# Shorter GpSimd pieces in the setup of an mLSTM and attention trunk, and a scale-and-shift bound behind the attention's last low part

## The chip, the cores and the metric

The kernel runs on one core of one Trainium2 chip. The metric is the device time of one execution in microseconds (us); a version's time is the median over several runs.

## The reference

Two layers over a residual stream x of 1024 tokens by 1024 features, float32. Layer A is an mLSTM block, layer B attends over one shared set of keys and values.

```python
def mlstm_layer(x, w_in, conv_w, conv_b, wq, wk, wv, w_if, b_if, gn_g, skip, w_out):
    xm, z, o_pre = jnp.split(x @ w_in, 3, axis=-1)           # 3 x 2048 columns
    xc = jax.nn.silu(causal_dwconv(xm, conv_w, conv_b))
    q, k, v = headwise(xc, wq), headwise(xc, wk), headwise(xm, wv)   # 4 x 4 blocks
    gates = jnp.concatenate([q, k, v], axis=-1) @ w_if + b_if
    ...                                                       # chunkwise mLSTM, 4 heads of 512
    y = (h.astype(x.dtype) + skip * xc) * jax.nn.silu(z)
    return y @ w_out

def dilated_attention_layer(x, w_in, w_out, kv_blocks, slopes):
    ...          # 3 groups (windows 128, 512, 2048; dilations 1, 4, 16), 8 heads of 128, ALiBi
    o = jnp.sum(wts[..., None] * jnp.stack(outs), axis=0)     # groups merged by their softmax sums
    y = o.astype(x.dtype) * jax.nn.silu(z)
    return y @ w_out

# reference(): after each layer
x = layer_norm(ALPHA * x + y, ln_g[layer], ln_b[layer])
# after layer A the stream is projected once to K and V for all groups
```

## The kernel before

**Products.** Every large product is done in three passes: an operand is split into a high part (ScalarE casts it, line 93) and a low part (VectorE subtracts the high part, line 94), and TensorE multiplies high by high, high by low and low by high (lines 98, 99, 100). The projections use a Strassen-like scheme (`strassen_steps`, `strassen_wide`): a weight matrix comes in four quarters, VectorE forms sums of them (lines 246, 250, 263, 264, 314), each sum or quarter is split and multiplied, and VectorE joins the results (lines 227, 233, 318). One 128-row product of such a scheme is 12 matmuls of 128x512.

**Order.** The program is traced once, top to bottom. A scheduler then sets the order of every engine's queue: at each moment of its own estimated timeline it takes, of the instructions of an engine that are ready, the one traced first. Work that is traced later but ready sooner slips ahead. The engines work off their queues strictly in that order, so an instruction that waits holds up all that stand behind it. `tc.issue_after(ins)` takes this freedom away: what is traced in its block on the engine of `ins` is queued behind `ins`. All DMAs are issued by SyncE (SP).

**Memory.** On-chip memory is cut by hand into 53 slots of 4 KB per partition (`self.slot(i)`). A new tile in a slot has to wait for the last reader or writer of the old one, DMAs included.

**The setup's tables.** In layer A, `setup()` runs beside the first projections. GpSimd builds there the block-diagonal matrices for v (`spread`, line 424, with 7, 7 and 2 columns of 128) and, three times, the product of a head-wise weight with the gate weights (`through`: line 431 multiplies, lines 432 and 433 add). The three times share one slot, 51, so the third load (`in_wifr`) waits until the second is done. ScalarE then copies the third result, eight columns at a time, into 16 tables (`A.copy` at line 461), which the first `values` matmuls of layer A (line 608) read. `setup_scores()`, some 300 us later, calls `through` once and `spread` twice with 8 columns, for the matrix that takes the place of q and k in layer A.

**The stored rows.** Layer A ends with a LayerNorm without its gain and shift; the eight row blocks of 128 tokens are kept in DRAM as layer B's residual, and need gain and shift (`scale_row`, lines 950 and 951, two VectorE instructions of 128x1024). Blocks 0 to 3 are treated in layer A. Blocks 4 to 7 are treated in layer B by `residual(tb)`: load into slot 52 (line 1098), scale, shift, store (line 1100). Gain and shift (`gain0`) lie in slots 50 and 51.

**Layer B's loop.** For each half of the heads (quad), each group g and each head h of the half: `queries_keys` (a Strassen scheme for q and k), `scores`, `attend`, in that order; `values(g, quad)` makes a group's values first, and `gates(1)` stands ahead of the third group's. `residual(4 + h)` is called for h = 0 to 3 at the end of each head of the second group (g = 1):

```python
qk = queries_keys(h, g, weigh_late)
p = scores(h, g, qk, stats[h])
...
kept[h] = attend(h, g, p, head_values(g, v, h % 4, h == 4))
if (quad, g) == (0, 1):
    residual(4 + h)
```

In this group `attend` transposes the softmax weights for four residues r (line 1286), splits each result straight from its bank (a low part of 128x256 on VectorE, line 94) and multiplies them with v (lines 98 to 100, and line 1309 for a part that isn't split). `self.last_split` is the low part that was traced last, so at the call it is that of r = 3 of this head. The group also keeps q and k whole for a part of the scores, in the same slot 52 (`whole`, written at line 1213, read at line 1261). After the fourth head, `values(2, 0)` loads eight blocks of value weights (line 1163), the first two into slots 50 and 51, the third into slot 52.

Of the kernel before, what the change touches and what calls it, by code (L numbers as in the profile page):

```python
# [14 lines left out]
ALU = mybir.AluOpType  # L15
# [3 lines left out]
P = 128  # L19
# [4 lines left out]
NC_A = INNER // P  # L24
# [37 lines left out]
class Kernel:  # L62
# [358 lines left out]

    def spread(self, dst, src, n):

        self.nc.gpsimd.tensor_tensor(dst.rearrange("p c (n j) -> p c n j", j=4),
                                     src.unsqueeze(2).to_broadcast([P, n, 32, 4]),
                                     self.mask.unsqueeze(1).unsqueeze(3).to_broadcast([P, n, 32, 4]), op=ALU.mult)

    def through(self, dst, w, rep, m):

        G = self.nc.gpsimd  # L430
        G.tensor_tensor(rep, rep, w.unsqueeze(3).to_broadcast([P, NC_A, 4, m]), op=ALU.mult)
        G.tensor_tensor(rep[:, :, 0:2], rep[:, :, 0:2], rep[:, :, 2:4], op=ALU.add)
        G.tensor_tensor(dst, rep[:, :, 0], rep[:, :, 1], op=ALU.add)

    def setup(self):
# [649 lines left out]
    def layer_b(self):  # L1085
        nc, tc, a, cp = self.nc, self.tc, self.a, self.cp
        V, A, G, T = nc.vector, nc.scalar, nc.gpsimd, nc.tensor
# [7 lines left out]
        def residual(tb):  # L1095

            r = self.slot(52)
            nc.sync.dma_start(r, self.dram["x1", tb])
            self.scale_row(r, *gain0)
            nc.sync.dma_start(self.dram["x1", tb], r)  # L1100

        jt = self.const("jt", [P, 384], tag="k1")
# [362 lines left out]
        gain0 = []  # L1465
# [45 lines left out]
        for quad in range(2):  # L1511
# [3 lines left out]
            for g in range(3):  # L1515
                if (quad, g) in gate_at:
                    self.w_raw = raw2
                    for n, _ in enumerate(gates(gate_at[quad, g], qk_slots[1::2])):
                        if n == 3:
                            weigh_late(h + 1)  # L1520
                v = values(g, quad)
                for h in heads:
                    qk = queries_keys(h, g, weigh_late)
                    p = scores(h, g, qk, stats[h])
                    if h == 7 and g == 2:
                        y6 = weigh_late(8)
                    if (quad, g) == (1, 0) and h < 7:
                        with self.tc.issue_after(self.last_split.ins):
                            fourth(h - 4)
                    if g == 2:  # L1530
                        if h == 7:
                            works = 44
                        fac = factors(h, stats[h])
# [3 lines that stand above are left out]
                    if g == 2:  # L1537
                        merge(h, *fac)
                        if late:
                            merged = h  # L1540
                        elif h < 7:
                            late = fetch_late(h)
# [8 lines left out]
        r = lambda i: self.slot(i, dtype=F32R)  # L1551
# [3 lines left out]
        for c in range(HB):  # L1555
# [12 lines left out]
            if c >= 6:  # L1568
                for i in range(2):
                    cs = slice(512 * i, 512 * i + 512)  # L1570
# [138 lines left out]
```

## Time and profile before

| | |
|---|---|
| median of 3 runs | 2009.45 us (2007.83 to 2010.1) |
| the profiled execution | 2008.7 us; its span, first to last instruction, 2006.9 us |
| mean granted TensorE clock | 0.994 |
| busy share | TensorE 98%, VectorE 72%, ScalarE 50%, GpSimd 8% |
| `spread` in `setup()`, from 90.31 us | 2 x 128x896 and 1 x 128x256 on GpSimd |
| `residual`'s four scales | at 1287.33, 1310.81, 1346.79 and 1368.55 us |

PE is TensorE (PEld its weight loads), DVE VectorE, ACT ScalarE, POOL GpSimd, SP SyncE. A timeline row reads: start, duration, engine, line, operation, tiles written and read (s is any slot, b any PSUM bank), partitions x elements and type, how many in a row; in brackets the idle time ahead of it and what ended that. A row of the chain that ended last reads: start, duration, what. Matmul durations are pipelined: in a full queue a 128x512 matmul takes 0.39 us and the next starts 0.23 us after it.

### The profile page before, as it was taken

How to read it: one execution, taken by the hardware profiler on the slowest of the kernel's cores; microseconds unless marked ns; L12 is line 12 of the kernel's file. 1: busy time of each engine (PE TensorE's matmuls, PEld its weight loads, DVE VectorE, ACT ScalarE, POOL GpSimd, SP SyncE). 2: the span in 40 equal slices, each digit the busy share in tenths (PEclk: the TensorE clock that was granted, in tenths of full speed). 3: DMA queues.
4: the chain of work that ended last, by engine and by line, in shares of the span. 5: the costliest groups of instructions: out<-in, count | busy, mean ns of one | idle time of the engine just before them, and what ended most of it. 6: DMA issues, size and time to landing. Idle time of an engine off the chain costs nothing.

```text
span 2006.9 us, 26588 instructions
## 1 busy us (share of the span) xinstructions
PE 1964.4 (98%) x9521; PEld 1630.7 (81%) x9521; DVE 1443.5 (72%) x2854; ACT 994.9 (50%) x1990; POOL 159.9 (8%) x127
## 2 busy tenths in 40 slices
PE   9999999999999999999999999999999999999997
PEld 7788888788888888878788888877888788888776
DVE  8678788676577776457866765686469887777978
ACT  5455555535745543343524642565256456666721
POOL 0110000022145343000000000000000000000000
PEclk9999999999999999999999999999999999999999
DMA  4445465456754543516121143224335532233743
GB/s 171 140 168 193 168 220 179 149 174 227 271 205 166 191 162 118 184 62 236 53 73 48 60 144 112 71 105 163 110 107 181 193 113 85 85 105 120 264 146 126
DMA packets 115900, 293.31 MB, mean 146 GB/s; under 512 B 13428, under 2 KB 31284, under 8 KB 115768
## 3 DMA queue, kind: packets, MB, share of 16 engines
q1 hardware_dynamic: 115768, 291.61, 41.6%
q8 instruction: 75, 1.23, 0.2%
q14 instruction: 57, 0.47, 0.1%
HBM read 202.65 MB, written 88.92 MB: 145 GB/s over the span
## 4 chain that ended last, share of the span: by engine, by line
PE 83%; DVE 9%; DMA 5%; ACT 2%; issue 1%; SPq 0%; DVEq 0%; ACTq 0%
PE b L98 26%; PE b L99 25%; PE b L100 25%; DVE s L94 3%; PE b L608 1%; PE b L1286 1%; DMA s<-df 1%; DMA ds<-s 1%; PE b L614 1%; PE b L884 1%; DMA s<-in_w_v 1%; PE b L1259 1%; DVE s L233 1%; PE b L1309 1%; ACT s L93 1%
## 5 line engine op out<-in xcount | busy, mean ns | idle before, releaser
L99 PE MATMUL b<-s,s 128*128 128x512 f32 (+3 forms) x2720 | 1037.3, 383 | 6.1 <-DVE s L94 6.0
L100 PE MATMUL b<-s,s 128*128 128x512 f32 (+3 forms) x2720 | 1023.2, 382 | 3.7 <-DVE s L94 3.7
L98 PE MATMUL b<-s,s 128*128 128x512 f32 (+2 forms) x2720 | 1003.4, 387 | 12.4 <-ACT s L93 9.8
L94 DVE TENSOR_TENSOR s<-s,s 128x512 fp32r<-128x512 f32 (+2 forms) x704 | 506.5, 735 | 290.4 <-ACT s L93 286.4
L93 ACT CAST s<-s 128x512 fp32r<-128x512 f32 (+2 forms) x708 | 437.3, 636 | 560.0 <-PE b L100 322.4
L98 PEld LDWEIGHTS b<-s,s 128*128 128x128 f32 x2720 | 513.0, 189 | 115.3 <-ACT s L93 16.3
L99 PEld LDWEIGHTS b<-s,s 128*128 128x128 f32 x2720 | 513.8, 189 | 104.4 <-DVE s L94 9.4
L100 PEld LDWEIGHTS b<-s,s 128*128 128x128 f32 x2720 | 511.2, 188 | 103.3 <-DVE s L94 6.9
L233 DVE TENSOR_TENSOR s<-s,b 128x512 f32<-128x512 f32 x132 | 89.8, 681 | 31.6 <-PE b L100 30.0
L1272 ACT ACTIVATE s<-s,nmax 128x128 f32<-128x128 f32 (+1 forms) x192 | 84.4, 441 | 39.4 <-DVE nmax L1270 38.8
L94 DVE TENSOR_TENSOR s<-b,s 128x512 fp32r<-128x512 f32 (+1 forms) x96 | 51.5, 551 | 32.5 <-ACT s L93 29.6
L573 DVE SCALAR_TENSOR_TENSOR s<-s,c_convw,s 128x512 f32<-128x512 f32 (+3 forms) x96 | 71.3, 754 | 3.1 <-ACT s L570 2.6
L227 DVE TENSOR_TENSOR s<-s,b 128x512 f32<-128x512 f32 x88 | 59.5, 679 | 16.4 <-PE b L100 13.0
L318 DVE TENSOR_TENSOR s<-s,b 128x512 f32<-128x512 f32 x100 | 63.1, 679 | 9.5 <-PE b L100 5.6
L818 ACT ACTIVATE s<-s,k 128x128 f32<-128x128 f32 x144 | 47.1, 392 | 40.9 <-DVE s L94 17.4
L1268 DVE CUSTOM_DVE_ANT_0 s<-b,k 128x128 f32<-128x128 f32 (+1 forms) x192 | 57.2, 344 | 7.8 <-PE b L100 6.7
L246 DVE TENSOR_TENSOR s<-s,s 128x512 f32<-128x512 f32 x44 | 30.2, 689 | 42.4 <-DMA s<-in_w_qk 16.8
L314 DVE TENSOR_TENSOR s<-s,s 128x1024 f32<-128x1024 f32 x40 | 49.4, 1248 | 13.8 <-DMA s<-in_w_v 9.3
L93 ACT CAST s<-b 128x512 fp32r<-128x512 f32 (+1 forms) x96 | 44.0, 480 | 18.2 <-PE b L100 12.8
L777 POOL TENSOR_TENSOR s<-s 128x512 fp32r<-128x512 f32 x32 | 44.4, 1403 | 75.2 <-ACT s L776 62.0
L1217 DVE SCALAR_TENSOR_TENSOR s<-s,s 128x512 fp32r<-128x512 f32 x48 | 42.4, 883 | 9.9 <-ACT s L1216 9.4
L888 POOL TENSOR_TENSOR s<-s,s 128x512 f32<-128x512 f32 x32 | 42.5, 1343 | 65.0 <-DVE s L887 48.9
(182 smaller groups left out, 1490.4 us busy)
## 6 DMA issues: line engine op xcount, KB each, us to landing
s<-in_w_qk SPq DMA_DIRECT2D x48, 512.0 KB
s<-in_w_out SPq DMA_DIRECT2D x40, 512.0 KB
dp<-s SPq DMA_DIRECT2D x32, 512.0 KB
s<-dp SPq DMA_DIRECT2D x32, 512.0 KB
s<-in_w_v SPq DMA_DIRECT2D x24, 512.0 KB
s<-df SPq DMA_DIRECT2D x24, 512.0 KB
dn<-s SPq DMA_DIRECT2D x20, 512.0 KB
s<-dn SPq DMA_DIRECT2D x20, 512.0 KB
```

What stands on the lines that cost most here:

```text
L93: self.nc.scalar.copy(h, src)
L94: self.last_split = (l_eng or self.nc.vector).tensor_tensor(l, src, f(h), op=ALU.subtract)
L98: mm(ps, lh, rh, start=start, stop=False, skip_group_check=skip)
L99: mm(ps, lh, rl, start=False, stop=False, skip_group_check=skip)
L100: mm(ps, ll, rh, start=False, stop=stop, skip_group_check=skip)
L227: self.last_plus = V.tensor_tensor(o, p, q, op=add)
L233: V.tensor_tensor(o, p[lane][rows], q[lane][rows], op=add)
L314: eng.tensor_tensor(o[j], p[j], q[j], op=op)
L318: V.tensor_tensor(o, p, q, op=add)
L573: V.scalar_tensor_tensor(u[i][:, lo:o + 512], xm[i][:, lo - s:o + 512 - s], convw[:, c, 3 - s:4 - s], u[i][:, lo:o + 512], op0=ALU.mult, o ...
L1268: V.tensor_tensor_reduce(out=dst, in0=sc, in1=bias, op0=ALU.add, op1=ALU.max, scale=1.0, scalar=-3e38, accum_out=mx[:, b:b + 1])
L1272: self.last_exp = A.activation(res[b][0], res[b][0], AF.Exp, bias=nm[:, b:b + 1], accum_out=stat[:, 1, g, b:b + 1])
```

## The change

1. `spread` and `through`, all on GpSimd: `spread` is done two columns of 128 at a time (at most 256 elements per partition). In `through` the multiplication is done in four pieces of four columns and the first addition in two pieces of eight columns; the last addition stays whole.
2. `residual`: `scale_row` is traced within `issue_after(self.last_split.ins)`, so VectorE gets the scale and the shift only behind the low part of r = 3 of the head that was just traced. The load and the store are not bound.

```diff
     def spread(self, dst, src, n):
-        self.nc.gpsimd.tensor_tensor(dst.rearrange("p c (n j) -> p c n j", j=4),
-                                     src.unsqueeze(2).to_broadcast([P, n, 32, 4]),
-                                     self.mask.unsqueeze(1).unsqueeze(3).to_broadcast([P, n, 32, 4]), op=ALU.mult)
+        for o in range(0, n, 2):
+            m = min(2, n - o)
+            self.nc.gpsimd.tensor_tensor(dst[:, o:o + m].rearrange("p c (n j) -> p c n j", j=4),
+                                         src[:, o:o + m].unsqueeze(2).to_broadcast([P, m, 32, 4]),
+                                         self.mask.unsqueeze(1).unsqueeze(3).to_broadcast([P, m, 32, 4]), op=ALU.mult)
     def through(self, dst, w, rep, m):
         G = self.nc.gpsimd
-        G.tensor_tensor(rep, rep, w.unsqueeze(3).to_broadcast([P, NC_A, 4, m]), op=ALU.mult)
-        G.tensor_tensor(rep[:, :, 0:2], rep[:, :, 0:2], rep[:, :, 2:4], op=ALU.add)
+        for o in range(0, NC_A, 4):
+            cs = slice(o, o + 4)
+            G.tensor_tensor(rep[:, cs], rep[:, cs], w[:, cs].unsqueeze(3).to_broadcast([P, 4, 4, m]), op=ALU.mult)
+        for o in range(0, NC_A, 8):
+            cs = slice(o, o + 8)
+            G.tensor_tensor(rep[:, cs, 0:2], rep[:, cs, 0:2], rep[:, cs, 2:4], op=ALU.add)
         G.tensor_tensor(dst, rep[:, :, 0], rep[:, :, 1], op=ALU.add)
...
             r = self.slot(52)
             nc.sync.dma_start(r, self.dram["x1", tb])
-            self.scale_row(r, *gain0)
+            with self.tc.issue_after(self.last_split.ins):
+                self.scale_row(r, *gain0)
             nc.sync.dma_start(self.dram["x1", tb], r)
```

## The prediction

> **What bounds the kernel now.** I read the page's busy shares first, then the windows by stage, then engine by engine the timeline of the two places that the change touches, and the chain that ended last.
>
> ```profile
> PE 1964.4 (98%) x9521; PEld 1630.7 (81%) x9521; DVE 1443.5 (72%) x2854; ACT 994.9 (50%) x1990; POOL 159.9 (8%) x127
> 95.00:100.00 5.00, 4.26 (x12) 3.35 (x13) 4.40 (x5) 1.69 (x4) 4.84 (x5) 0.66 0.01 5
> 100.00:105.00 5.00, 5.00 (x24) 4.10 (x23) 2.75 (x4) 2.44 (x5) 2.33 (x5) 1.00 0.74 250
> 400.00:450.00 50.00, 50.00 (x223) 41.38 (x222) 37.85 (x52) 17.94 (x30) 13.12 (x7) 1.00 0.54 182
> 1320.00:1330.00 10.00, 8.92 (x32) 7.21 (x33) 8.72 (x15) 8.11 (x14) 0.00 (x0) 0.83 0.14 56
> ```
>
> TensorE is busy for 98% of the span, so only what opens or closes a hole in it, or lowers its granted clock, counts. The windows (length, then PE, PEld, DVE, ACT and POOL busy, then PE's clock) show such a hole beside GpSimd's tables at 95 to 100 us, clock 0.66, and one beside the stored rows at 1320 to 1330, clock 0.83. Beside the second table-making, near 410 us, TensorE is busy throughout: there the shorter pieces can gain nothing.
>
> **GpSimd's tables at 90 us.** The timelines of VectorE, GpSimd and TensorE (start, us, engine, line):
>
> ```profile
> 87.21 0.69 DVE L246 TENSOR_TENSOR s<-s,s 128x512 f32<-128x512 f32 x1 [3.51 <-DMA s<-in_w_z]
> 90.31 3.80 POOL L424 TENSOR_TENSOR s<-s,em 128x896 f32<-128x896 f32 x2 [89.87 <-DMA s<-in_wvT]
> 90.43 2.13 DVE L250 TENSOR_TENSOR s<-s 128x512 f32<-128x512 f32 x1
> 92.59 2.07 DVE L263 TENSOR_TENSOR s<-s,s 128x512 f32<-128x512 f32 x1
> 94.58 1.10 DVE L94 TENSOR_TENSOR s<-s,s 128x512 fp32r<-128x512 f32 x1
> 93.27 0.50 PE L98 MATMUL b<-s,s 128*128 128x512 f32 x1 [0.23 <-ACT s L93]
> 95.74 0.49 PE L100 MATMUL b<-s,s 128*128 128x512 f32 x1 [1.74 <-DVE s L94]
> 96.95 0.63 PE L98 MATMUL b<-s,s 128*128 128x512 f32 x1
> 99.51 0.60 PE L98 MATMUL b<-s,s 128*128 128x512 f32 x1
> ```
>
> A VectorE subtraction of 128x512 takes 0.69 us alone; the two that meet the two 896-column pieces take 2.13 and 2.07. The first ends at 92.56, some 0.4 after the first piece (half of 3.80 after 90.31), so I read that each waits for the piece in progress and then runs. TensorE needs their results: it idles 0.23 and 1.74 us, and then runs slowly: starts 96.95 and 99.51 are six matmuls apart, 0.43 us each where 50/223 = 0.22 is usual at 400 us; about eight such cost 8 x 0.2 = 1.6. The hole costs 0.23 + 1.74 + 1.6 = 3.6 us.
>
> ```profile
> 105.81 1.09 POOL L431 TENSOR_TENSOR s<-s,s 128x512 f32<-128x512 f32 x1 [0.58 <-DMA s<-in_wifr]
> 410.60 0.65 POOL L431 TENSOR_TENSOR s<-s 128x256 f32<-128x256 f32 x1 [301.70 <-DMA s<-in_wqT]
> 101.88 0.46 POOL L462 TENSOR_TENSOR k<-k 128x128 f32<-128x128 f32 x1
> 108.12 0.78 POOL L433 TENSOR_TENSOR k<-s 128x128 f32<-128x128 f32 x1
> 109.94 0.68 ACT L461 COPY s<-k 128x8 f32<-128x8 f32 x6
> 110.52 0.62 ACT L93 CAST s<-s 128x512 fp32r<-128x512 f32 x1
> ```
>
> After the change no piece has more than 256 columns: 0.65 us by the 256-column row (a product of the same kind). The three VectorE steps from 90.43 then cost at most 3 x (0.65 + 0.65) = 3.9 and end by 94.3 rather than 95.7; waiting half a piece each, by 93.4. TensorE wants the last near 93.7 (two matmuls after 93.27), so 0 to 0.5 us of idling stays where 1.97 was, and I let the slow clock go with it: 3.6 - 0.5 = 3.1 gained. The bounds are 3.6 and, if the waits merely spread, 0.
>
> Pieces cost fixed time. From 128 columns in 0.46 and 512 in 1.09, a column costs 0.0016 and an instruction 0.25. The first setup goes from 3 spreads and 9 steps to 4 + 4 + 1 pieces and 3 x 7 steps: 18 more, 4.5 us on GpSimd. (The second has 10 more, 2.5 us under a busy TensorE: nothing.) The third table, now done at 108.9, would come near 113.4, and later if each extra piece also waits for a VectorE step. Behind it wait ScalarE's 16 copies (from 109.94), and behind those in ScalarE's queue the cast at 110.52 that feeds TensorE. The copies are placed anew for longer tables, so I take 0.5 us lost, between 0 and the rival's price below. Part one: 2.6 gained.
>
> **The stored rows.** Four rows are scaled and shifted, one per head. The first two heads:
>
> ```profile
> 1290.67 1.21 DVE L951 TENSOR_TENSOR s<-s,s 128x1024 f32<-128x1024 f32 x1
> 1292.87 0.39 PE L99 MATMUL b<-s,s 128*128 128x256 f32 x1 [0.37 <-DVE s L94]
> 1295.07 0.60 ACT L1213 ACTIVATE s<-b 128x512 f32<-128x512 f32 x1
> 1299.57 0.42 DVE L94 TENSOR_TENSOR s<-b,s 128x256 fp32r<-128x256 f32 x1
> 1301.86 0.39 PE L1261 MATMUL b<-s 128*128 128x128 f32 x2
> 1310.89 1.13 DVE s L950
> 1313.92 5.69 DMA s<-in_w_qk
> 1319.73 0.69 DVE s L246
> 1316.97 0.42 DVE L94 TENSOR_TENSOR s<-b,s 128x256 fp32r<-128x256 f32 x1 [0.77 <-ACT s L93]
> 1321.08 0.50 PE L98 MATMUL b<-s,s 128*128 128x512 f32 x1 [1.79 <-DVE s L233]
> 1324.82 0.63 PE L99 MATMUL b<-s,s 128*128 128x512 f32 x1
> ```
>
> On the chain that ended last, the second head's scale (1310.89, 1.13 us) stands ahead of the low parts whose ends free the weight slots; the weight load starts at 1313.92 and lands 5.69 later; TensorE idles 1.79 and then runs about eight slow matmuls (the 0.63 at 1324.82 is the last), 1.6 again. With the scale behind the last low part (1316.97), the load starts 1.13 sooner and the hole shrinks to 0.66. Scale and shift (1.23 + 1.21) then run from about 1316.3, in VectorE's wait for that load, so they cost nothing unless the load lands before 1318.7. I take 1.1 plus half of the slow clock, 0.8: 1.9 gained (bounds 0 and 3.4). At the first head the 0.37 wait goes.
>
> What the move delays: the row sits in slot 52, where the next head's whole query and key are written (ScalarE, 1295.07), read by the scores from 1301.86. The last low part now ends at 1299.99, or about 1297 without the row ahead of it; 2.4 of VectorE and some 3.2 of store (the store is issued at the shift's end, 1291.88, and 1295.07 is the write) give 1302.6 to 1305.6, so those scores start 2 to 5 us later. Other products fill that time; I take 0.5 lost (bounds 0 and 3). SyncE's queue holds the row's store, which moves by as much.
>
> ```profile
> 1346.79 1.23 DVE L950 TENSOR_TENSOR s<-s,s 128x1024 f32<-128x1024 f32 x1 [0.30 <-DMA s<-dx]
> 1348.67 0.50 PE L100 MATMUL b<-s,s 128*128 128x512 f32 x1 [0.34 <-DVE s L94]
> 1353.05 0.49 PE L1309 MATMUL b<-pw,s 128*128 128x128 f32 x2 [0.21 <-ACT pw L1297]
> 1368.55 1.23 DVE s L950
> 1369.80 6.12 DMA s<-in_w_v
> 1376.02 1.14 ACT L93 CAST s<-s 128x512 fp32r<-128x512 f32 x2 [4.47 <-DMA s<-in_w_v]
> 1375.27 0.33 SPq L1163 DMA_DIRECT2D s<-in_w_v  x1
> 1379.41 0.42 DVE L94 TENSOR_TENSOR s<-b,s 128x256 fp32r<-128x256 f32 x1
> 1382.83 0.38 PE L1309 MATMUL b<-pw,s 128*128 128x128 f32 x2
> ```
>
> At the third head 0.34 + 0.21 go. The fourth costs. Gain and shift lie in slots 50 and 51, which the next value weights overwrite: that load starts at 1369.80, the moment the fourth scale ends, and ScalarE's first cast waits for it until 1376.02. Bound behind the low part of 1379.41, the scale would end at 1381.06 and the load land at 1387.2; SyncE's later issues (1375.27) stand behind it. But that low part is late because its cast stands behind the waiting cast of 1376.02; freed, it ends near 1375 and the load lands near 1381 to 1382. TensorE has other work until 1380 to 1383 (the last attention product is at 1382.83). Loss: 0 to 4.6 (1387.2 and 0.6 of cast against 1383.2), and a slow clock behind the larger; I take 2.0, nearer to the freed order. Part two: 0.4 + 1.9 + 0.5 - 0.5 - 2.0 = 0.3 gained.
>
> **Sum.** 2.6 + 0.3 = 2.9 us off the profiled execution's 2008.7 (span 2006.9 and 1.8 around it) is 2005.8. That execution is 0.75 below the median of 2009.45, so the same step from the median gives 2006.5. Less than 0.2% (4.0 us) either way can't be told from no change: 2005.4 to 2013.5 counts as the same.
>
> The slow stretches follow holes of 1.74 and 1.79 us. The Trainium skill (TensorE: Matmul & The Clock Gate, section "What's actually happening") has the clock halved only after an idle window of about 3.4 us; by that the holes here would not cause the dips, and closing them would not return the 1.6 and 0.8: 2008.9. The trace differs, with dips behind both shorter holes, so I keep the terms.
>
> **Rivals.**
> *Both parts pay.* The fourth head's value load is hidden, since the profile shows the late cast that holds its low part back; 2.0 comes back, and the second dip goes whole (0.8): 2003.7. Against it: the load is already waited for.
> *The value load is late.* 4.6 + 1.6 instead of 2.0: 2006.5 + 4.2 = 2010.7. It decides once the fourth head's last low part ends after about 1376. For it: 1369.80 follows the scale without a gap.
> *The clock dips stay* although the holes close (their cause is not shown): 2008.9.
> *Slower: ScalarE blocks on the tables.* A 128-column step takes 0.78 us among VectorE's (108.12) and 0.46 alone, so it waited 0.3; a whole VectorE step is 0.69. If each of the 18 added pieces waits so, they cost 18 x (0.25 + 0.3 to 0.69) = 10 to 17 us; the third table ends at 119 to 126, and copies still placed near 110 hold up the cast behind them, and TensorE with it for 8 to 15 us: 2014 to 2021, say 2016. It decides once the copies wait over 7 us. Against it: the copies are placed by the new lengths.
> *No effect: the waits merely spread.* VectorE and GpSimd exclude each other for the same columns in all, so VectorE loses as much in more and shorter waits, and the 3.1 is not gained: 2009.6; the rest of the order is also planned anew, worth a few us either way. For it: the sum of the columns is unchanged. Against it: TensorE waited for one result, not for the sum. In the Trainium skill (SBUF — State Buffer, section "SBUF: two separate sides") the shared port is held for a whole instruction and the other engine fully blocks; the trace agrees with 2.13 beside 0.69.
>
> **How the numbers follow.** Forecast 0.40 (its own range 2003.5 to 2009.5), both pay 0.20, late load 0.12, dips stay 0.08, ScalarE blocks 0.12, no effect 0.08. The likeliest is 2006.5. Faster by over 0.2%: both pay (0.20), two fifths of the forecast (0.16) and 0.03 of the rest: 0.39. Slower: the blocked case (0.12), and 0.06 of late load and no effect: 0.18. The same: 0.43. The range from 2001.5 to 2013.5 leaves out the blocked case and small tails, at most 0.2.
>
> **What would show it.** Right: at 90 to 100 us no VectorE step over 1.4 us, no TensorE wait over 0.6, clock above 0.9; no wait of 1.8 near 1320; scale rows only behind the heads' low parts. Wrong: ScalarE idle for GpSimd near 110 us; a TensorE hole over 2 us near 1380 behind the value load, or near 1300 behind the whole query; new holes where nothing was changed.

## The result, and the profile after

The changed kernel takes 2019.01 us (median of 5 runs, 2016.96 to 2021.29), the kernel before beside it 2007.83 (2004.17 to 2010.1): a ratio of 1.0058, 95% interval 1.0046 to 1.0071, so 11 to 12 us slower. The forecast was 2006.5 with a range up to 2013.5; the time lies above the range. The profiled execution is the slowest of the five, 2021.29 us; its span is 2019.5 (before 2006.9), its mean granted clock 0.992 (before 0.994).

Where the time went is read from the same stretches of both traces. First the windows of the kernel before (length, then PE, PEld, DVE, ACT, POOL busy with their counts, PE's clock, DMA share, GB/s), then those of the changed kernel:

```profile
1270.00:1300.00 30.00, 29.63 (x152) 24.99 (x151) 23.45 (x51) 18.44 (x41) 0.00 (x0) 1.00 0.20 70
1300.00:1330.00 30.00, 27.74 (x144) 23.35 (x143) 21.88 (x54) 19.98 (x50) 0.00 (x0) 0.94 0.30 106
1330.00:1360.00 30.00, 29.45 (x155) 24.86 (x154) 20.47 (x48) 17.50 (x40) 0.00 (x0) 1.00 0.20 70
1360.00:1400.00 40.00, 38.24 (x187) 30.69 (x186) 29.39 (x61) 21.31 (x53) 0.00 (x0) 1.00 0.58 198
```

```profile
1270.00:1300.00 30.00, 30.00 (x158) 25.66 (x157) 24.29 (x52) 17.98 (x41) 0.00 (x0) 1.00 0.15 53
1300.00:1330.00 30.00, 24.72 (x122) 19.52 (x121) 16.98 (x47) 17.27 (x46) 0.00 (x0) 0.94 0.25 88
1330.00:1360.00 30.00, 27.16 (x137) 21.67 (x136) 20.57 (x51) 17.98 (x44) 0.00 (x0) 1.00 0.25 88
1360.00:1400.00 40.00, 33.11 (x154) 26.83 (x153) 27.53 (x59) 19.42 (x45) 0.00 (x0) 0.87 0.58 203
```

TensorE idles 4.9 us in these 130 us before (130 less the four PE times) and 15.0 after: 3.0 more at 1300 to 1330, 2.3 at 1330 to 1360, 5.1 at 1360 to 1400, where the clock also falls to 0.87. One line of layer B's scores dates this (its matmuls with their number, ns min/median/max, first and last start), before and after:

```profile
L1261 PE MATMUL b<-s x64: 270/273/275, 1276.5 to 1798.2; 128*128 128x128 f32 x64
```

```profile
L1269 PE MATMUL b<-s x64: 270/273/276, 1276.6 to 1810.9; 128*128 128x128 f32 x64
```

The first is 0.1 us later, the last 12.7. All of the 12.6 us of span arises between them; the first part of the kernel, with GpSimd's tables in it, ends in this execution where it ended before.

The holes, from TensorE's timeline of the changed kernel (in brackets the idle time ahead and what ended it):

```profile
1303.55 0.79 PE L98 MATMUL b<-s,s 128*128 128x512 f32 x1 [2.56 <-ACT s L1221]
1324.17 0.50 PE L98 MATMUL b<-s,s 128*128 128x512 f32 x1 [1.86 <-DVE s L233]
1354.22 0.50 PE L98 MATMUL b<-s,s 128*128 128x512 f32 x1 [1.35 <-DVE s L233]
1392.66 2.07 PE L98 MATMUL b<-s,s 128*128 128x512 f32 x4 [5.99 <-ACT s L93]
```

The first is new and ends with the write of the whole query (line 1221; it was 1213). The chain that ended last, with start, duration and what ran, shows how it comes about:

```profile
1297.36 0.42 DVE s L94
1297.78 1.14 DVE s L957
1298.95 1.24 DVE s L958
...
1300.20 2.61 DMA dx<-s
...
1302.89 0.60 ACT s L1221
...
1303.55 0.79 PE b L98
```

The last low part of the first head, scale (957), shift (958), the row's store to DRAM, the next head's whole query into the same slot 52, and then TensorE, which needs the bank that this write reads. Six steps, each waiting for the one ahead. The chain goes through the next weight load (line 180), which now starts 3.15 us later than the 1313.92 of before, not 1.13 sooner, and the wait behind it is 1.86 where it was 1.79:

```profile
1317.07 5.63 DMA s<-in_w_qk
```

At the fourth head the chain is another one, through the value weights, as scale, load, cast and matmul:

```profile
1384.24 0.42 DVE s L94
1384.66 1.13 DVE s L957
...
1386.32 5.59 DMA s<-in_w_v
...
1391.99 0.63 ACT s L93
...
1392.66 2.07 PE b L98 x4
```

That load started at 1369.80 before. The cast that waits for it stands at 1391.99 against 1376.02.

### The profile page after: what moved, and what is told of

Same layout as the page of the kernel before. It is cut to its first block, busy times and chain, and to the rows that moved or that the text cites. A ratio compares the mean times of both kernels' runs of the same rounds, so it can differ in the third digit from the quotient of the medians.

```text
span 2019.5 us, 26587 instructions
## 1 busy us (share of the span) xinstructions
PE 1968.4 (97%) x9521; PEld 1633.8 (81%) x9521; DVE 1440.0 (71%) x2854; ACT 994.9 (49%) x1990; POOL 168.7 (8%) x155
## 4 chain that ended last, share of the span: by engine, by line
PE 78%; DVE 10%; DMA 7%; ACT 3%; issue 2%; POOL 1%; SPq 0%; DVEq 0%; ACTq 0%
PE b L98 24%; PE b L100 24%; PE b L99 24%; DVE s L94 3%; DMA s<-df 2%; PE b L615 1%; PE b L1294 1%; ACT s L93 1%; DMA s<-in_w_out 1%; PE b L621 1%; PE b L891 1%; DVE s L1276 1%; DMA s<-in_w_qk 1%; DMA s<-in_w_z 1%; DVE s L233 1%
## 5 line engine op out<-in xcount | busy, mean ns | idle before, releaser
L314 DVE TENSOR_TENSOR s<-s,s 128x1024 f32<-128x1024 f32 x40 | 49.5, 1249 | 11.9 <-DMA s<-in_w_v 7.7
```

What stands on the lines that cost most here:

```text
L314: eng.tensor_tensor(o[j], p[j], q[j], op=op)
```

## The experiments

Ratios are to the kernel before on the same chip, each with its 95% interval of 0.0010 to 0.0018 to either side; a difference of two of them is uncertain by some 0.0017, or 3.4 us.

**The two parts apart.** `pieces` has the diff's changes of `spread` and `through` alone, `bind` that of `residual` alone.

> Only GpSimd's shorter pieces; the stored rows as in the kernel before. Theory (all of the 12.6 us of span come from the stored rows: in the changed kernel the first score matmul of layer B, at 1276.4 us, is 0.1 later than before, the last at 1810.8 is 12.7 later): 2005 to 2009 us, ratio to before 0.998 to 1.000; the TensorE wait of 1.74 us near 95 us is gone and the wait near 1380 us is as in the kernel before. Rival (GpSimd's longer third table, done at 113.2 us rather than 108.9, and the new plan behind it carry the loss): over 2014 us, ratio above 1.003.

> Only the scale and shift bound behind the last low part of each head; GpSimd's pieces as in the kernel before. Theory: 2018 to 2022 us, ratio 1.005 to 1.007, with the whole query and key of heads 1 to 3 written 8, 13 and 10 us later than before and the first cast of the next value weights near 1392 us. Rival (GpSimd's pieces carry the loss): 2006 to 2011 us, ratio within 0.002 of 1.

Measured: `pieces` 2008.3 us, ratio 0.9989 (0.9977 to 1.0000), some 2.2 us gained. `bind` 2022.64 us, 1.0063 (1.0045 to 1.0080), as slow as both together. The loss is that of the bound rows; the rival with GpSimd's longer table is out. VectorE and TensorE of `pieces` at GpSimd's tables, and the window behind:

```profile
90.31 1.09 DVE L250 TENSOR_TENSOR s<-s 128x512 f32<-128x512 f32 x1
91.44 0.99 DVE L263 TENSOR_TENSOR s<-s,s 128x512 f32<-128x512 f32 x1
89.61 0.50 PE L98 MATMUL b<-s,s 128*128 128x512 f32 x1 [0.72 <-ACT s L93]
```

```profile
95.00:100.00 5.00, 5.00 (x23) 4.13 (x22) 3.28 (x5) 1.76 (x4) 5.00 (x9) 1.00 0.52 162
```

The subtractions of 2.13 and 2.07 us are now 1.09 and 0.99, the 0.72 is the last wait before 101 us, and the window that had 4.26 at clock 0.66 has 5.00 at 1.00.

**The fourth row alone unbound**, the other three as in the change (`three`):

```diff
-            with self.tc.issue_after(self.last_split.ins):
+            with self.tc.issue_after(self.last_split.ins) if tb < 7 else ExitStack():
```

> Both parts of the change, but the fourth row (behind the fourth head) is not bound, so gain and shift leave slots 50 and 51 as early as the plan allows. By the trace of the changed kernel TensorE is idle 15.0 us between 1270 and 1400 us (4.9 before): 2.6 more for heads 2 and 3 up to 1330, 2.3 more up to 1360, 5.1 more at 1360 to 1400 and some 3.6 in a slow clock there. Theory (each bound row costs by itself, the fourth most): 2009 to 2013 us, first value cast before 1388 us. Rival (the first three heads carry it, the fourth only passes their delay on): 2016 to 2020 us.

Measured: 2016.54 us, ratio 1.0029 (1.0017 to 1.0040). That is the time that the rival gave, but not its reason alone: against `pieces` the first three binds cost 0.40%, some 8 us, and the fourth another 0.29%, some 6.

**The row in a tile of its own** (`row_apart`):

```diff
-            r = self.slot(52)
-            nc.sync.dma_start(r, self.dram["x1", tb])
+            r = self.t(cp, [P, 768], tag="rx")
+            nc.sync.dma_start(r, self.dram["x1", tb][:, 0:768])
...
```

> Both parts of the change, but the row has a tile of its own instead of slot 52, so the next head's whole query and key need not wait for the row's store; the tile holds 768 columns, and the last 256 columns of rows 4 to 7 are left without gain and shift. Scale and shift are a quarter shorter, 0.9 us each. Theory (what the bind costs at the first three heads is the wait of the whole query for the store, through slot 52): the whole queries are written within 4 us of the kernel before, 2.5 to 3.5 us of idling at 1300 to 1360 go, and what is left is the fourth row's value load: 2010 to 2015 us. Rival (the low part itself comes late, or VectorE's order does it, and slot 52 only reports it): 2017 to 2021 us.

Measured: 2009.5 us, ratio 0.9994 (0.9982 to 1.0007), with all four rows bound. Its windows, then TensorE, VectorE and ScalarE at the fourth head:

```profile
1300.00:1330.00 30.00, 30.00 (x169) 26.07 (x168) 25.44 (x60) 21.05 (x50) 0.00 (x0) 1.00 0.32 107
1330.00:1360.00 30.00, 30.00 (x159) 25.71 (x158) 23.47 (x63) 20.09 (x49) 0.00 (x0) 1.00 0.25 89
1360.00:1400.00 40.00, 30.73 (x144) 25.07 (x143) 21.04 (x38) 16.91 (x41) 0.00 (x0) 0.87 0.47 173
```

```profile
1372.37 0.40 PE L1317 MATMUL b<-pw,s 128*128 128x128 f32 x2
1380.90 2.08 PE L98 MATMUL b<-s,s 128*128 128x512 f32 x4 [8.13 <-ACT s L93]
1371.50 0.42 DVE L94 TENSOR_TENSOR s<-b,s 128x256 fp32r<-128x256 f32 x1 [0.76 <-ACT s L93]
1380.22 1.14 ACT L93 CAST s<-s 128x512 fp32r<-128x512 f32 x2 [6.35 <-DMA s<-in_w_v]
```

The idling at 1300 to 1360 is gone, also that of the kernel before: slot 52 was the link. One thing that I expected did not come: the whole queries are not written near their old times. The second head's stands at 1283.46 where the kernel before has 1295.07, so not only a wait went; the order moved too. This row is also a quarter shorter (0.95 us for the scale against 1.14); whole rows follow in `apart_free`, `tile_only` and `whole_three`. What is left is one hole of 8.13 us at the value weights. The heads run ahead so well that the last attention product is at 1372.37, and nothing is left to do until the load that waited for the fourth row has landed.

**That hole.** `apart_three` is `row_apart` with the fourth row unbound; `apart_swap` is `row_apart` with the first quarter of the value weights in slots 48 and 49 and the third in 50 and 51.

```diff
-            ... ((50, 51), (52, 46), (48, 49), (14, 15)))[g]
+            ... ((48, 49), (52, 46), (50, 51), (14, 15)))[g]
```

> As the run with the row in a tile of its own (768 of 1024 columns of rows 4 to 7 scaled and shifted), but the fourth row is not bound. There TensorE idled nothing from 1270 to 1360 us and then 8.13 us at one place (1372.8 to 1380.9), waiting for value weights whose slots 50 and 51 hold gain and shift until the fourth row is done. Theory (the bind on the fourth row makes that wait): the wait falls to some 2 us as in the kernel before, its slow clock (some 2 us) with it: 1999 to 2004 us, ratio to before 0.994 to 0.997. Rival (the value load is late for another reason, its own 6 us or SyncE's queue): 2007 to 2011 us, the wait stays over 6 us.

> As the run with the row in a tile of its own, all four rows bound, but the first quarter of the next value weights is loaded into slots 48 and 49 and the third into 50 and 51. Theory (slots 50 and 51 hold up the first quarter): its load starts before 1370 us and the wait near 1381 falls from 8.13 to under 5 us: 2003 to 2008 us, 2 to 6 us under the run it is taken from. Rival (the products need sums of all quarters, so whichever quarter lies there holds up the same product): the wait stays at 7 us or more, no change in time.

Measured: `apart_three` 1996.88 us, ratio 0.9944 (0.9932 to 0.9957); `apart_swap` 2001.36 us, 0.9961 (0.9947 to 0.9974). From 1270 to 1500 us TensorE of `apart_three` has no hole at all:

```profile
1270.00:1500.00 230.00, 230.00 (x1145) 194.59 (x1145) 157.98 (x349) 121.75 (x267) 0.00 (x0) 1.00 0.33 113
```

With the swap the row is bound as late as in `row_apart`, yet the longest wait is 1.19 us; ScalarE's first cast starts at 1374.64 and not 1380.22:

```profile
1374.64 1.14 ACT L93 CAST s<-s 128x512 fp32r<-128x512 f32 x2 [1.06 <-DMA s<-in_w_v]
```

So it was not the late row as such, but gain and shift in the two slots that the first quarter wanted. Both runs came out some 2 us below the ranges that I had given.

**Single rows in slot 52.** Bound only behind the second head (`second_only`, `tb == 5`) or only behind the fourth (`fourth_only`, `tb == 7`), with the shorter pieces:

> GpSimd's shorter pieces, and of the four rows only the second (behind the second head) is bound; the row lies in slot 52. The prediction gave this bind 1.9 us gained by an earlier weight load, with bounds 0 and 3.4, and nothing lost: 2003 to 2006 us, ratio to before 0.996 to 0.999. Theory now (the third head's whole query waits for the row's store, and with it the score, the next weight load and TensorE): 2 to 6 us slower than the pieces alone, 2009 to 2014 us, ratio 1.000 to 1.003, with a TensorE wait on the whole query near 1360 us.

> GpSimd's shorter pieces, and of the four rows only the fourth (behind the fourth head) is bound; no whole query follows it, so only gain and shift in slots 50 and 51 count. The prediction's term: 2.0 us lost (bounds 0 and 4.6 with a slow clock). Theory now, from the runs with and without this bind (0.29% with the row in slot 52, 0.50% with a tile of its own): 6 to 10 us slower than the pieces alone, 2012 to 2017 us, ratio 1.002 to 1.004, with one TensorE wait of 6 to 9 us near 1380. Rival (in the order of the kernel before other work covers it): 2006 to 2010 us.

Measured: `second_only` 2013.24 us, ratio 1.0022 (1.0010 to 1.0035), 0.33% above `pieces`; `fourth_only` 2015.47 us, 1.0026 (1.0014 to 1.0037), 0.37% above. The first is ScalarE and TensorE of `second_only`, the second TensorE of `fourth_only`:

```profile
1334.39 0.60 ACT L1221 ACTIVATE s<-b 128x512 f32<-128x512 f32 x1 [1.16 <-DMA dx<-s]
1323.64 0.50 PE L98 MATMUL b<-s,s 128*128 128x512 f32 x1 [2.02 <-DVE s L233]
1383.07 0.39 PE L99 MATMUL b<-s,s 128*128 128x256 f32 x1 [2.34 <-DVE s L94]
```

```profile
1388.89 2.08 PE L98 MATMUL b<-s,s 128*128 128x512 f32 x4 [5.68 <-ACT s L93]
```

The third head's whole query waits for the store, at 1334 us and not near 1360 as I had expected. The hole that this bind was to shrink did not shrink (2.02), and 2.34 us at the fourth head is new: there the unbound fourth row stands ahead of a low part. How much of the 0.33% is the link and how much the new order, this run does not tell. The fourth bind costs some 7 us also when the rows before it are not bound.

**No bind, the row in a tile of its own.** `apart_free` has the shorter pieces, `tile_only` the pieces as before; both scale the whole row. The small table `jt2` is loaded behind the last row's store.

```diff
-            r = self.slot(52)
+            r = self.t(cp, [P, 1024], tag="rx")
...
-        jt2 = self.const("jt2", [P, P], tag="k3")
...
+                    with self.tc.issue_after(self.last_row.ins):
+                        late_jt2.append(self.const("jt2", [P, P], tag="k3"))
```

> GpSimd's shorter pieces, no bind at all, and the whole row of 1024 columns in a tile of its own instead of slot 52 (to make room, one small table is loaded later). Theory (the bind and the own tile are both needed: the tile takes away the wait for the store, the bind the scale that stands ahead of the low parts): the wait of 1.8 us near 1320 stays, 2004 to 2009 us. Rival (slot 52 was the cost already before the change, and an own tile alone does it): 1999 to 2004 us, no wait over 1 us from 1270 to 1360.

> The kernel before with one thing changed: rows 4 to 7 in a tile of their own rather than slot 52 (one small table loaded later to make room); no bind, GpSimd's pieces as before. Theory (link through slot 52 cost the kernel before its 4.9 us of idling from 1270 to 1400; the pieces are worth 2 us more): 2002 to 2006 us, ratio 0.997 to 0.999, no TensorE wait over 1 us from 1270 to 1400. Rival (the gain with pieces and own tile together came from the new plan of the whole kernel): 2006 to 2010 us.

Measured: `apart_free` 2001.75 us, ratio 0.9966 (0.9954 to 0.9979); `tile_only` 2005.54 us, 0.9978 (0.9968 to 0.9988). Each fills the stretch; first `apart_free`, then `tile_only`:

```profile
1270.00:1500.00 230.00, 230.00 (x1145) 194.52 (x1145) 152.73 (x343) 121.14 (x259) 0.00 (x0) 1.00 0.28 94
```

```profile
1270.00:1500.00 230.00, 230.00 (x1138) 194.29 (x1137) 151.40 (x322) 121.17 (x258) 0.00 (x0) 1.00 0.28 95
```

My theory for `apart_free` fell: the bind is not needed to close the holes. The hole of 1.79 us near 1320, which the prediction put down to the scale ahead of the low parts, closes with the tile alone. `tile_only` differs from the kernel before in the tile (and the table loaded late) only, and there the second head's whole query is written 11.9 us behind the first head's whole key (1278.75 to 1290.63), where it was 23.1 (1271.94 to 1295.07).

**Two whole versions with the bind.** `halves_three` takes each row in two halves through one tile of 512 columns; `whole_three` takes 768 columns bound and 256 unbound, each part in a tile of its own. Both leave the fourth row unbound. The diff is that of `whole_three`; the other has two slices of 512, one tag and `tb < 7` for both.

```diff
+            for ds, tag, late in ((slice(0, 768), "rx", tb < 7), (slice(768, D), "ry", False)):
+                r = self.t(cp, [P, ds.stop - ds.start], tag=tag)
...
+                with self.tc.issue_after(self.last_split.ins) if late else ExitStack():
+                    self.scale_row(r, *[t[:, ds] for t in gain0])
...
```

> A whole version: GpSimd's shorter pieces; rows 4 to 7 scaled and shifted in two halves of 512 columns each, through one tile of 512 columns of its own; bound behind the last low part for the first three heads only. Theory (the own tile breaks the link with the whole query, the unbound fourth row frees the value load): 2000 to 2005 us, ratio 0.995 to 0.998. Rival (two loads and two stores per row through one tile make SyncE wait for the first store and hold up weight loads behind it): 2008 us or more.

> A whole version: GpSimd's shorter pieces; rows 4 to 7 in two parts with a tile each, 768 columns bound behind the last low part for the first three heads, 256 columns not bound. Theory (no link through slot 52, gain and shift released early): 1996 to 2001 us, ratio 0.994 to 0.997, no wait from 1270 to 1400. Rival (the second part's load, store and two VectorE steps stand ahead of what TensorE needs): 2003 us or more; or the fourth row's second part comes behind the value weights' sums, as in the halves, and a wait of over 10 us appears near 1385.

Measured: `halves_three` 2020.55 us, ratio 1.0057 (1.0041 to 1.0072). SyncE, VectorE, ScalarE and TensorE at its fourth head:

```profile
1377.90 0.43 SPq L1107 DMA_DIRECT2D rx<-dx  x1
1385.95 0.68 DVE L957 TENSOR_TENSOR rx<-rx,s 128x512 f32<-128x512 f32 x1
1390.09 1.14 ACT L93 CAST s<-s 128x512 fp32r<-128x512 f32 x2 [11.52 <-DMA s<-in_w_v]
1390.76 2.07 PE L98 MATMUL b<-s,s 128*128 128x512 f32 x4 [13.29 <-ACT s L93]
```

The second half of the fourth row is loaded only at 1377.90 and scaled at 1385.95, and so long gain and shift keep their slots: a TensorE wait of 13.29 us. The rival's time, but by the value weights again and not by weight loads held up in SyncE's queue. `whole_three`: 1999.66 us, ratio 0.9948 (0.9933 to 0.9963). It computes everything, and against the changed kernel it is 0.9948/1.0058 = 0.989. Its stretch is full too:

```profile
1270.00:1500.00 230.00, 230.00 (x1145) 194.54 (x1144) 158.04 (x348) 122.05 (x270) 0.00 (x0) 1.00 0.35 116
```

Whether three bound rows gain anything beside the tile is not shown: `whole_three` is 0.0018 below `apart_free`, about as much as such a difference is uncertain by.

## Why the prediction failed, step by step

**GpSimd's pieces: the sum about right, two of its terms not.** 2.6 us were forecast, 2.2 measured, and the interval reaches from no gain to 4.6; `apart_free` against `tile_only`, which differ in the pieces alone, gives 2.4, uncertain by some 3.2. In `pieces` the steps at 90 to 100 us are those foreseen, and no wait is left there at all: the 3.6 us that it put on the hole went whole, and not 3.1 of them. The other term, for ScalarE's copies, was too small. The third table was put near 113.4; in `pieces` it ends at 112.24, ScalarE waits 2.52 us for it, and the delay goes on through ScalarE's cast, VectorE (line 580) and ScalarE again (line 584) to TensorE, which idles 1.43 us where the kernel before idles nothing:

```profile
112.27 1.48 ACT L468 COPY s<-k 128x8 f32<-128x8 f32 x14 [2.52 <-POOL k L440]
120.95 0.63 ACT L584 ACTIVATE s<-s 128x512 f32<-128x512 f32 x1 [0.63 <-DVE s L580]
121.67 0.47 PE L98 MATMUL b<-s,s 128*128 128x512 f32 x1 [1.43 <-ACT s L584]
```

The chain that ended last runs through these steps; from 104 to 123 us in the kernel before it stays on TensorE. The forecast had 0.5 us for this: 3.6 - 1.4 is 2.2, so that the sum came out near is in part luck. It is the blocked ScalarE of the rivals, at 1.4 us and not 8 to 15. This wait is 1.00 to 1.46 us in nine of the eleven profiles with short pieces, and 0.30 and 0.41 in the two (the changed kernel and `apart_swap`) in which TensorE had lost time at 90 us:

```profile
90.55 0.50 PE L98 MATMUL b<-s,s 128*128 128x512 f32 x1 [1.72 <-ACT s L93]
```

```profile
90.00:95.00 5.00, 4.45 (x11) 3.23 (x12) 4.37 (x5) 2.27 (x4) 4.00 (x5) 0.66 0.80 277
```

These are a row and a window of the changed kernel: a slow stretch stood there all the same, behind a wait of 1.72 us (0.72 in `pieces`) that was over before GpSimd's first piece, at 91.00; so this execution shows nothing of the gain.

**The whole query behind the store: the time right, the price wrong.** The prediction gave 1302.6 to 1305.6 for the row to be out of slot 52; the write came at 1302.89. It then said that other products fill the time, 0.5 us lost, at most 3, beside gains of 2.8 at the first three heads. This step failed. No other product filled the time: TensorE's next one needs the bank that the waiting write reads (2.56 us); the scores behind it set the next weight load, and each head hands its delay on. The first three binds cost some 8 us (`three` against `pieces`).

**The second head's hole: wrong cause.** The gain of 1.9 us rested on the scale at 1310.89 being what made the weight load late. With the bind the load came 3.15 us later. The 0.8 for the slow clock behind this hole rested on one execution: in `pieces` the wait at the same product is 2.22 us and no slow matmul follows. With the bind and no link, and with no bind and no link, the hole is gone: it went with slot 52, and the kernel before paid for that too. By which of the slot's waits the old hole arose I have not traced; with the tile the whole order is also planned anew.

**The fourth head: the low part and the load partly right, the cover wrong.** The prediction had the low part near 1375 and the load landed at 1381 to 1382 if the low part was freed from standing behind the waiting cast; if not, the load at 1387.2. TensorE was to have other work until 1380 to 1383, read from the attention product at 1382.83 before. The heads are shifted against each other in these kernels, so each is put here on the times of the kernel before by the start of its fourth head's last score matmul (1364.39 before, 1370.96 in the changed kernel, 1368.47 in `fourth_only`, 1362.93 in `row_apart`):

| | low part ends | load lands | last attention product starts |
|---|---|---|---|
| before | 1379.8 | 1375.9 | 1382.8 |
| changed kernel | 1378.1 | 1385.3 | 1379.7 |
| `fourth_only` | 1376.9 | 1384.1 | 1378.7 |
| `row_apart` | 1373.4 | 1381.7 | 1373.8 |

With slot 52 the low part came forward by 2 to 3 us and not 5, and the load landed between the two cases. With the tile both came as forecast. But that attention product stands behind the very low part that was freed, and in each kernel it comes forward at least as far as the low part. The cover came forward with the thing it was to hide. Nor was all of that cover other work. From 1377.79 on, once the first value cast was done, 18 matmuls of 128x512 stand before 1382.83 in the kernel before, some 4 us, which by their order look like the value products themselves. The rows do not name their slots, so this is a reading and not shown; if it holds, that work could never have covered the load it needs.

In place of 2.0 us the bind costs 6 (`three` against the change), 7 (`fourth_only` against `pieces`) or 10 (`apart_three` against `row_apart`), each uncertain by some 3.

Of the rivals, the late value load had the fourth head's price right (4.6 + 1.6 = 6.2 us) and its condition too: the low part ends after 1376 in the changed kernel and in `fourth_only`. The gains beside it did not come. The holes near 1380 and near 1300, by which the prediction said that it would be proved wrong, are the two that made the loss; the third sign, ScalarE idle for GpSimd near 110 us, came as well, at a small price.

## What to carry to other kernels

Before an instruction is bound later, follow its buffer and the buffers that it reads to their next writers: the price is paid there, by the engine that wants the buffer next, and by the bank and the queue behind that write. Work that is to hide a wait must not itself depend on what is moved; if it does, it comes forward too and the wait lies bare. Where a chain goes from step to step through one buffer, a second buffer takes the wait away and the order need not be touched: with a tile of its own for the row, TensorE had no hole in that stretch with the first three rows bound and with none bound.

## What the runs showed of the hardware

A granted clock that falls behind a hole has no fixed price per hole. TensorE's waits of 1.72 us (changed kernel, 90.55) and 1.74 (before, 95.74) were followed by seven or more matmuls at some 0.43 us each, but one of 2.78 us in `three` by none; there the next starts come 0.34 and 0.23 us later, the 0.23 of a full queue. At one and the same product near 1320 the wait of 1.79 us before was followed by a slow stretch, and that of 2.22 in `pieces` (last row) by none:

```profile
1303.81 0.50 PE L98 MATMUL b<-s,s 128*128 128x512 f32 x1 [2.78 <-ACT s L1221]
1304.15 0.40 PE L99 MATMUL b<-s,s 128*128 128x512 f32 x1
1304.38 0.39 PE L100 MATMUL b<-s,s 128*128 128x512 f32 x1
1322.67 0.50 PE L98 MATMUL b<-s,s 128*128 128x512 f32 x1 [2.22 <-DVE s L233]
```

The waits of over 5 us (5.99 here, 8.13, 5.68, 13.29) were all followed by slow matmuls. The Trainium skill (TensorE: Matmul & The Clock Gate, section "What's actually happening") says that the window by which the clock is judged is free-running, 3.4 us long. That fits a short hole that costs at one time and not at another. That a whole idle window is needed, as the prediction took it from there, does not fit the dips behind 1.72 and 1.74.
